# Two seven-product blocks per MLP, with weights split two pieces at a time

## The chip, the cores and the metric

The kernel runs on one core of one Trainium2 chip. The metric is device time in microseconds (us) of one execution; lower is better. Before the change three runs gave 847.58, 847.60 and 848.07 us, median 847.6. The engines are PE (matrix products), DVE (element-wise on tiles), ACT (element-wise with functions), POOL, and SP, which here only issues transfers.

## What is computed

A two-layer encoder on 256 tokens of 1024 channels, all in float32. Each layer has a token mixer (pooling, dilated attention, gates) and a gated MLP; only the MLP is touched in depth:

```python
def _conv_ffn(xn, w_up, conv_w, conv_b, w_down):
    a, gval = jnp.split(xn @ w_up, 2, axis=-1)          # 256 x 1024 times 1024 x 5632
    a = depthwise_conv_width_3(a, conv_w) + conv_b       # neighbours along the tokens
    return (jax.nn.gelu(a) * gval) @ w_down              # 256 x 2816 times 2816 x 1024

for layer in range(2):
    h = h + _token_mixer(_rmsnorm(h, norm1[layer]), ...)
    h = h + _conv_ffn(_rmsnorm(h, norm2[layer]), ...)
```

## The kernel before

**Precision by splitting.** Products run on 32-bit operands in a rounded format. To keep float32 accuracy every weight piece is split in two: ACT copies the raw piece into `wh` (rounded), DVE subtracts, `wl = raw - wh`. A product of a piece is then three products: x-high by wh, x-high by wl, x-low by wh. A *piece* is 128 x 1024 elements, half of a 1 MB load of one raw buffer. There are three raw buffers (`RAW`) and five pairs of split buffers (`BUFS`).

**Class Weights** holds the list of loads and the list of pieces in the order in which PE uses them. `get()` hands PE the next piece and first calls `_split` for the pieces up to four ahead, as far as split buffers are free. A split is ACT's copy, then whatever waits in `W.between` (DVE work of the moment), then DVE's subtraction. `load` issues a transfer on SP's queue, up to three raw buffers ahead; that transfer waits on the queue until its buffer is free. `bring_back` issues the second half of a crossing (below), right after the next weight load.

**The MLP's groups.** `w_up` has 5632 columns: branch a (2816) and branch g (2816), in groups of 512 columns, ("a", n) and ("g", n), n = 0 to 4, and a last group ("b", 20) with 256 of each. A plain group has 4 pieces, each with 12 products of 128 x 512 (`by_tokens`, `v_sum`). `w_down` is used in 22 pieces, also 12 products each (`residual_mm`, "d"). The order is that of `MLP_GROUPS`.

**The block ("w", 3)** computes a3 and g3 together. The 2 x 2 arrangement of (weight half, branch) needs eight products of quadrants; Strassen's identity makes it seven: 11, T1, 22, T2, 21, T3, T4, each in two units of 6 products of 128 x 512 (`halves_of_block`). T1 to T4 are differences of quadrants that DVE makes in place in the raw tile (`use_block`, L344), before they are split. Between them stand units "d" (`BLOCK`). DVE adds the banks afterwards (`add`, L1692).

**Crossings.** Convolution needs channels on partitions and tokens along the row. `to_z`/`turn` transpose a group's two results on DVE (two instructions at L852), `send` writes them to DRAM (L857), and four reads (L864) bring them back in the other layout.

**Convolution.** For each pair of 128-channel chunks f = 0, 2, ..., 20 five steps run: `fetch_up` (6 ACT instructions), `neighbours` (2 DVE), `activate` (ACT, gelu), `gate` (DVE), `keep_up` (ACT copy, then a DVE subtraction). Chunks f and f+1 belong to group f // 4. A *place* is one unit of PE work, counted through the MLP; place 8 is the first unit after the groups a0 and g0. `PAIR_PLACES` gives (p1, p3) for each f: `fetch_up` at p1, `neighbours` and `activate` at p1 + 1, `gate` and `keep_up` at p3. `at_place` puts `neighbours` and `gate` into `W.between`: if the unit of that place splits a piece, they run on DVE between ACT's copy and DVE's subtraction, else after the unit. The ACT steps and the end of `keep_up` come behind the unit.

From place 8 on the MLP is in a hand-written order (`manual_schedule`): every engine takes its instructions in the order in which the program names them.

Of the kernel before, what the change touches and what calls it, by code (L numbers as in the profile page):

```python
# [52 lines left out]
    ("11", 0), ("11", 1), "d", ("T1", 0), ("T1", 1), "d", "d", ("22", 0), ("22", 1), "d", ("T2", 0), ("T2", 1), "d",  # L53
    ("21", 0), ("21", 1), "d", ("T3", 0), ("T3", 1), "d", "d", ("T4", 0), ("T4", 1),
# [64 lines left out]
class Weights:  # L119
# [6 lines left out]
    RAW, BUFS, LOOK = 3, 5, 3  # L126

    def __init__(self, tc, pool, idle, small):
# [7 lines left out]
        self.between = []  # L136
# [3 lines left out]
        self.sums = {}  # L140

    def add(self, src, shape, cuts, tag=None):

        n = len(self.loads)
        self.loads.append((src, shape, tag))
        return [(n, cut, c_shape) for cut, c_shape in cuts]

    def use(self, pieces, slots=()):
        slots = list(slots) + [None] * len(pieces)
        self.pieces += [p + (slot,) for p, slot in zip(pieces, slots)]  # L150

    def ahead(self, i):


        upto = min(n for n, *_ in self.pieces[i : i + 3])
# [52 lines left out]
    def _split(self, upto):  # L208
        nc = self.nc
        first = self.n_split  # L210
        while self.n_split < len(self.pieces):
            i = self.n_split
            n, cut, shape, slot = self.pieces[i]
            if i >= upto and (slot is None or i >= max(upto, first + 2) or i >= upto + 4 or i < 4):
                break
            if slot is None and len(self.live) == self.BUFS:
                break
            self.load(n + 1)
            with ExitStack() as queued:
                for insts, some in self.later:  # L220
                    for inst in insts if i in some else ():
# [6 lines left out]
                if i in self.sums:  # L228
                    self.sums.pop(i)()
            self.load(self.ahead(i))  # L230

    def run_between(self):

        while self.between:
            self.between.pop(0)()

    def open_next(self):
# [3 lines left out]
        n, cut, shape, slot = self.pieces[i]  # L241
        if slot is None:
            self.live.add(i)
            h, l = (
                self.pool.tile([P, *shape], F32R, tag=tag, bufs=self.BUFS, name=f"{tag}{i}")
                for tag in ("wh", "wl")
            )
# [44 lines left out]
    def free(self, i):  # L292
        self.live.discard(i)


@with_exitstack
def encoder(ctx, tc, x, w_in, w_pool, pool_scale, w_a, w_b, w_o, norm1, norm2, w_up, conv_w,
# [32 lines left out]
    def use_block(units, made, first):  # L330
# [9 lines left out]
        def sum_later(i, name, j):  # L340

            def make():
                one, other = terms[name]
                nc.vector.tensor_sub(out=raw(name, j), in0=raw(one, j), in1=raw(other, j))  # L344
# [3 lines left out]
        for j in range(2):  # L348
            sum_later(len(W.pieces) + first + j, "T1", j)
        behind = [u for u in units if len(u) > 2]  # L350
        for unit in units:
            if len(unit) > 2:
                W.use([unit])
                behind = behind[1:] or behind
                continue
            name, j = unit
            if name in SUMS:
                sum_later(len(W.pieces), SUMS[name], j)
            if name in ("22", "21"):
                W.use([made[name][j]])  # L360
            else:
                W.use([(behind[0][0], lambda t, name=name, j=j: raw(name, j), (2, 512))])

    def first_quadrants(w, n):
        return {
            "11": quadrant(w, 0, DFF + n * 512, "ybig"), "12": quadrant(w, 0, n * 512, "at2"),
        }

    def block(w, down, n, made):
        made = dict(made)  # L370
        d = rows(down, 0) + rows(down, 2 * P)
        made["22"] = quadrant(w, 1, n * 512)
        d += rows(down, 4 * P)
        made["21"] = quadrant(w, 1, DFF + n * 512)
        d += rows(down, 6 * P)
# [1391 lines left out]
```

## Time and profile before

| | |
|---|---|
| median of three runs | 847.6 us |
| the profiled execution's own time | 848.11 us |
| its span, first to last instruction | 846.3 us |
| MLP of layer 0, from the group g0 on | about 257.6 to 425 us |
| MLP of layer 1, from the group g0 on | about 673.9 us to the end |
| granted TensorE clock | 0.999 |
| transfers | 214.02 MB, 253 GB/s |

The page of the profile gives busy time for each engine and the chain of work that ended last. The view by windows gives the busy time of each engine in chosen stretches; the timeline lists instructions in order, with the idle time before each and what ended it; the view of waits sums that up. Two consecutive instructions of an engine overlap in the trace by about 0.1 us, so what an instruction costs in a full queue is the distance between starts and not its length.

### The profile page before, as it was taken

To read this page: it belongs to the slowest core of one execution; us is meant where nothing else is said; L and a number is where in the kernel's file an instruction comes from. 1 tells how busy PE (TensorE), PEld (TensorE's weight loads), DVE (VectorE), ACT (ScalarE), POOL (GpSimd) and SP (SyncE) were. 2 spreads that over 40 slices of the span, in tenths; PEclk is the share of its full clock that TensorE was granted. 3 is DMA by queue.
4 is the path that set the end of the run, shared out by engine and by line. 5 is a ranking of instruction groups with operands and counts; after the bars stand their busy time and mean duration, and the time that the engine had idled before them with its cause. 6 is when DMAs were issued, how large, how long until landed. Compare 5 with 4: busy or idle time off the path is not lost.

```text
span 846.3 us, 10959 instructions
## 1 busy us (share of the span) xinstructions
PE 838.7 (99%) x3889; PEld 699.3 (83%) x3889; DVE 665.5 (79%) x860; ACT 531.1 (63%) x770; POOL 35.5 (4%) x96
## 2 busy tenths in 40 slices
PE   9999999999999999999999999999999999999997
PEld 7888888888888887888888888888888888888886
DVE  6968877757767799788898997868577867998884
ACT  7744556655554776488765555577455647757883
POOL 1720000000010000000000000000000100000000
PEclk9999999999999999999999999999999999999999
DMA  8699987796759886889857669968777499768861
GB/s 305 211 304 289 317 282 251 246 282 218 233 206 302 276 275 199 256 264 316 272 185 225 222 225 316 284 235 261 247 261 269 164 308 309 227 224 275 303 218 50
DMA packets 147967, 214.02 MB, mean 253 GB/s; under 512 B 7801, under 2 KB 69185, under 8 KB 147913
## 3 DMA queue, kind: packets, MB, share of 16 engines
q1 hardware_dynamic: 147480, 212.67, 76.8%
q10 hardware_dynamic: 432, 0.66, 0.2%
q8 instruction: 30, 0.49, 0.2%
q14 instruction: 25, 0.20, 0.1%
HBM read 186.02 MB, written 27.28 MB: 252 GB/s over the span
## 4 chain that ended last, share of the span: by engine, by line
PE 90%; DMA 3%; DVE 3%; ACT 2%; issue 1%; POOL 0%; ACTq 0%; SPq 0%; DVEq 0%; POOLq 0%
PE t_ps L798 54%; PE res_ps L716 6%; PE res_ps L715 6%; PE res_ps L717 6%; PE t_ps L917 4%; PE v_ps L798 3%; DMA raw<-in_w_up_dram 3%; PE v_ps L1101 3%; PE v_ps L917 2%; PE pool_ps L702 1%; PE v_ps L1000 1%; PE o_ps L1392 1%; PE s_ps L1344 1%; ACT wh L259 1%; DVE wl L261 1%; PE s_ps L1339 1%
## 5 line engine op out<-in xcount | busy, mean ns | idle before, releaser
L261 DVE TENSOR_TENSOR wl<-raw,wh 128x1024 fp32r<-128x1024 f32 x292 | 350.9, 1219 | 92.4 <-ACT wh L259 91.7
L798 PE MATMUL t_ps<-wh,x 128*128 128x512 f32 x1280 | 401.8, 390 | 0.0
L259 ACT CAST wh<-raw 128x1024 fp32r<-128x1024 f32 x292 | 302.1, 1048 | 158.8 <-PE t_ps L798 71.2
L798 PEld LDWEIGHTS t_ps<-wh,x 128*128 128x128 f32 x1280 | 240.3, 188 | 50.0
L798 PE MATMUL t_ps<-wl,x 128*128 128x512 f32 x640 | 249.0, 389 | 0.0
L798 PEld LDWEIGHTS t_ps<-wl,x 128*128 128x128 f32 x640 | 120.2, 188 | 24.7
L715 PE MATMUL res_ps<-wh,actq 128*128 128x512 f32 (+1 forms) x184 | 70.0, 380 | 0.0
L716 PE MATMUL res_ps<-wl,actq 128*128 128x512 f32 (+1 forms) x184 | 69.8, 380 | 0.0
L717 PE MATMUL res_ps<-wh,actk 128*128 128x512 f32 (+1 forms) x184 | 69.3, 380 | 0.0
L798 PE MATMUL t_ps<-wh,po 128*128 128x512 f32 x128 | 41.4, 395 | 0.0
L715 PEld LDWEIGHTS res_ps<-wh,actq 128*128 128x128 f32 x184 | 34.6, 188 | 6.7
L716 PEld LDWEIGHTS res_ps<-wl,actq 128*128 128x128 f32 x184 | 34.6, 188 | 6.7
L717 PEld LDWEIGHTS res_ps<-wh,actk 128*128 128x128 f32 x184 | 34.6, 188 | 6.5
L1604 ACT ACTIVATE a<-zga,prm 128x256 f32<-128x256 f32 x80 | 38.9, 512 | 0.0
L592 POOL TENSOR_SCALAR ss<-ss 128x1 f32<-128x1 f32 x8 | 3.1, 386 | 764.2 <-ACT junk L585 764.2
L344 DVE TENSOR_TENSOR raw<-raw,raw 128x1024 f32<-128x1024 f32 x24 | 29.3, 1222 | 0.0
L798 PEld LDWEIGHTS t_ps<-wh,po 128*128 128x128 f32 x128 | 24.0, 188 | 4.9
L715 PE MATMUL res_ps<-wh,m 128*128 128x512 f32 (+1 forms) x72 | 26.5, 368 | 0.0
L716 PE MATMUL res_ps<-wl,m 128*128 128x512 f32 (+1 forms) x72 | 26.3, 365 | 0.0
L717 PE MATMUL res_ps<-wh,m 128*128 128x512 f32 (+1 forms) x72 | 26.0, 365 | 0.0
L1608 DVE TENSOR_TENSOR y<-y,a 128x510 f32<-128x510 f32 x22 | 14.9, 679 | 13.6 <-ACT y L1602 13.6
L798 PE MATMUL t_ps<-wl,po 128*128 128x512 f32 x64 | 24.9, 390 | 0.0
(221 smaller groups left out, 1069.6 us busy)
## 6 DMA issues: line engine op xcount, KB each, us to landing
raw<-in_w_in_dram SPq DMA_DIRECT2D x58, 1024.0 KB
raw<-in_w_up_dram SPq DMA_DIRECT2D x40, 1024.0 KB
raw<-in_w_down_dram SPq DMA_DIRECT2D x22, 1024.0 KB
crossing<-crossing SPq DMA_DIRECT2D x22, 512.0 KB
crossing<-way SPq DMA_DIRECT2D x16, 512.0 KB
raw<-in_w_a_dram SPq DMA_DIRECT2D x8, 1024.0 KB
raw<-in_w_o_dram SPq DMA_DIRECT2D x8, 1024.0 KB
zga<-crossing SPq DMA_DIRECT2D x40, 128.0 KB
```

The lines of the kernel that those rows point to most:

```text
L259: inst = nc.scalar.copy(out=h, in_=src)
L261: inst = self.rests[i] = nc.vector.tensor_sub(out=l, in0=src, in1=h.bitcast(F32))
L344: nc.vector.tensor_sub(out=raw(name, j), in0=raw(one, j), in1=raw(other, j))
L702: nc.tensor.matmul(out, w(k), x, start=(steps is first and k == 0), stop=(steps is last and k == nk - 1), skip_group_check=turns["rest"],)
L715: nc.tensor.matmul(ps, ah, wh, start=first, stop=False, skip_group_check=on)
L716: nc.tensor.matmul(ps, ah, wl, start=False, stop=False, skip_group_check=on)
L717: nc.tensor.matmul(ps, al, wh, start=False, stop=last, skip_group_check=on)
L798: nc.tensor.matmul(ps, x2[:, 2 * n + j, part, t, :], w[:, j, :], start=(n + m == 0), stop=(n == last and m == 5),)
L917: nc.tensor.matmul(ps, operands[name](part, 2 * j + c), w[:, c, :], start=(name in ("11", "T1") and j + m == 0), stop=(j == 1 and m == 5), ...
L1101: nc.tensor.matmul(ps[t], a[:, k, t, :], w[:, j, :], start=(k + m == 0), stop=(k == KD - 1 and m == 2),)
L1604: nc.scalar.mul(out=out, in_=a, mul=row(j, c))
L1608: nc.vector.tensor_add(out=y[:, :, 1:], in0=y[:, :, 1:], in1=t["a0"][:, :, : S - 1])
```

## The change

Per MLP there are two blocks, groups 1 and 3, in place of one; the groups g2 and b run inside the first, the first eight pieces of `w_down` inside the second. Two pieces of the same load are split by one ACT and one DVE instruction of 128 x 2048 (`W.two`). There are six split slots in place of five, taken in neighbouring pairs. A load is issued when a raw buffer is given back, not ahead of that, and the quadrants of the second block are loaded once those of the first are used up (`not_before`). The sums T1 to T4 are made whole. In the block, ACT's copies of banks come ahead of a split (`at_once`). The places of the convolutions change. The bias table of the attention holds two heads at a time and is loaded again for the other two.

```diff
 MLP_GROUPS = (
-    ("g", 0), ("a", 1), ("g", 1), ("a", 2), ("g", 2), ("w", 3), ("b", 20), ("a", 4), ("g", 4),
-    ("d", 8), ("d", 12), ("d", 16), ("d", 20),
+    ("g", 0), ("a", 2), ("w", 1), ("a", 4), ("w", 3), ("g", 4), ("d", 8), ("d", 12), ("d", 16), ("d", 20),
 )
+BETWEEN = {1: (("g", 2), ("b", 4 * NQ)), 3: (("d", 0), ("d", 4))}

 PAIR_PLACES = (
-    (11, 14), (14, 16), (19, 22), (21, 23), (46, 48), (49, 51), (52, 54), (55, 57), (60, 62), (63, 65), (58, 60),
+    (9, 13), (11, 15), (35, 38), (41, 45), (22, 25), (26, 29), (60, 64), (63, 66), (65, 69), (68, 71), (70, 73),
 )

 BLOCK = (
-    ("11", 0), ("11", 1), "d", ("T1", 0), ("T1", 1), "d", "d", ("22", 0), ("22", 1), "d", ("T2", 0), ("T2", 1), "d",
-    ("21", 0), ("21", 1), "d", ("T3", 0), ("T3", 1), "d", "d", ("T4", 0), ("T4", 1),
+    ("11", 0), ("11", 1), "d", "d", ("T1", 0), ("T1", 1), "d", "d", ("22", 0), ("22", 1), "d", "d",
+    ("T2", 0), ("T2", 1), "d", "d", ("T3", 0), ("T3", 1), ("21", 0), ("21", 1), ("T4", 0), ("T4", 1),
 )
...
-    RAW, BUFS, LOOK = 3, 5, 3
+    RAW, SLOTS, LOOK = 3, 6, 3
...
     def ahead(self, i):
+        if self.two:
+            upto = end = self.n_loaded
+            held = sum(
+                tag is None and self.last_use[n] > i
+                for n, (_, _, tag) in enumerate(self.loads[:upto]) if n > upto - 10
+            )
+            while held < self.RAW and end < len(self.loads) and self.not_before.get(end, i) <= i:
+                end += 1
+                if self.loads[end - 1][2] is None:
+                    held += 1
+                    upto = end
+            return upto
...
     def _split(self, upto):
...
+            count = 1
+            if self.makes_two(i):
+                if self.two_slots() is not None:
+                    count = 2
+                elif i >= self.n_got + 2:
+                    break
...
-                for hi, lo, *_ in self.open_next():
+                for hi, lo, *_ in self.open_next(count):
+                    self.run_at_once()
                     hi()
                     self.run_between()
                     lo()
...
     def open_next(self, count=1):
...
+            if count == 2:
+                h, l = (s[:, at : at + 2].rearrange("p s c -> p (s c)") for s in self.slots)
+                src = whole(self.raw[n]).rearrange("p k c -> p (k c)")
+                self.n_split += 2
+                def both(n):
+                    if n == 0:
+                        return nc.scalar.copy(out=h, in_=src)
+                    inst = nc.vector.tensor_sub(out=l, in0=src, in1=h.bitcast(F32))
...
-                nc.vector.tensor_sub(out=raw(name, j), in0=raw(one, j), in1=raw(other, j))
+                nc.vector.tensor_sub(out=whole(name), in0=whole(one), in1=whole(other))
...
+                if kind2 == "w":
+                    name, tag, c0 = (("11", "ybig", DFF), ("12", "at2", 0))[j]
+                    if corner:
+                        W.not_before[len(W.loads)] = W.last_use[corner[name][0][0]]
+                    made[name] = quadrant(w_up[l], 0, c0 + n2 * 512, tag)
...
-    bt = const.tile([P, HPG, NT * P], F32, name="bt")
+    bt = const.tile([P, 2, NT * P], F32, name="bt")
...
+    def load_bias(first, queue=nc.sync):
...
+        else:
+            visits["u", 1, 2] = ((load_bias, 0),)
...
-            4: ((W.bring_back,), (scores, 1)),
+            4: ((W.bring_back,), (scores, 1), (load_bias, 2, nc.scalar)),
...
         def at_place(p, make, *first):
+            W.at_once = [step for step in first if step in by_scalar]
+            first = [step for step in first if step not in by_scalar]
...
             def add(t):
                 m = kept["m"][:, t]
                 nc.vector.tensor_add(out=m, in0=bank("q"), in1=m)
-                turn("a", t, m)
+
+            def add_last():
+                add(1)
+                for t in range(2):
+                    turn("a", t, kept["m"][:, t])
+
+            by_scalar.extend((keep_first, keep_fifth, keep_both))
             after = {
                 "11": (keep_first,), "T1": (keep_fifth,), "22": (keep_both,), "T2": (lambda: add(0),),
-                "T3": (lambda: add(1),), "T4": (lambda: turn("g", 0, bank("p")), lambda: turn("g", 1, bank("q"))),
+                "T3": (add_last,), "T4": (lambda: turn("g", 0, bank("p")), lambda: turn("g", 1, bank("q"))),
             }
```

After an entry of `BLOCK` has been computed, the steps that `after` names for it run in the next unit. In the new order, places 8 to 11 are a2, 12 to 33 the first block, 34 to 37 a4, 38 to 59 the second block, 60 to 63 g4, and 64 on the pieces of `w_down` from the eighth.

More of the change, by code (lines that the diff above doesn't have):

```diff
@@ L140, in __init__ @@
         self.sums = {}
+        self.slots = [pool.tile([P, self.SLOTS, 1024], F32R, tag=tag, name=tag) for tag in ("wh", "wl")]
+        self.freed = {slot: slot - self.SLOTS for slot in range(self.SLOTS)}
+        self.slot_of, self.n_freed = {}, 0
     def add(self, src, shape, cuts, tag=None):
@@ L227, in _split, with run_at_once, makes_two @@
                     lo()
-                if i in self.sums:
-                    self.sums.pop(i)()
-            self.load(self.ahead(i))
+                for j in range(i, i + count):
+                    if j in self.sums:
+                        self.sums.pop(j)()
+            self.load(self.ahead(i + count - 1))
+    def run_at_once(self):
+        while self.at_once:
+            self.at_once.pop(0)()
     def run_between(self):
+        self.run_at_once()
         while self.between:
             self.between.pop(0)()
-    def open_next(self):
+    def makes_two(self, i):
+        if not self.two or i < self.n_scaled or i + 1 >= len(self.pieces):
+            return False
+        (*_, whole, slot), (*_, whole2, slot2) = self.pieces[i : i + 2]
+        return slot is None and slot2 is None and bool(whole) and whole2 is False
@@ L1545, in encoder @@
         run(attended)
-        g1 = gain(norm1[l + 1] if l + 1 < DEPTH else norm_f)
+        W.two = True
         acts = {}
```

163 lines of the change are left out of this document (99 added, 64 removed), and 10 rows, old and new, of the table VALUES.

## The prediction, as recorded before the run

> **What bounds the kernel now.** I read the page first: engine shares, then the chain that ended last.
>
> ```profile
> span 846.3 us, 10959 instructions
> PE 838.7 (99%) x3889; PEld 699.3 (83%) x3889; DVE 665.5 (79%) x860; ACT 531.1 (63%) x770; POOL 35.5 (4%) x96
> PE 90%; DMA 3%; DVE 3%; ACT 2%; issue 1%; POOL 0%; ACTq 0%; SPq 0%; DVEq 0%; POOLq 0%
> ```
>
> PE is busy almost throughout, but its lengths overlap, so this alone doesn't prove that it is never late. The chain in order of time gives the real pace:
>
> ```profile
> 438.30 5.44 PE t_ps L798 x24
> 443.74 1.36 PE v_ps L917 x6
> ```
>
> 24 products take 5.44 us: 0.2267 us each. A plain unit of 12 costs 2.72 us, a block unit of 6 costs 1.36. Then the windows: g0 to block, block, behind it, in layer 0.
>
> ```profile
> 257.60:317.60 60.00, 60.00 (x265) 49.36 (x263) 47.31 (x55) 39.63 (x57) 0.00 (x0) 1.00 0.89 293
> 317.60:358.70 41.10, 40.69 (x180) 33.62 (x180) 36.62 (x36) 22.59 (x25) 0.00 (x0) 1.00 0.70 225
> 358.70:417.50 58.80, 58.80 (x262) 48.70 (x262) 49.24 (x59) 50.71 (x82) 0.00 (x0) 1.00 0.87 282
> ```
>
> Columns are the stretch, its length, PE, PEld, DVE, ACT, POOL (busy and count), clock, DMA share, GB/s. 265 products at 0.2267 are 60.1 us: the first stretch is full, and so is the third. The block holds 180 products, 40.8 of 41.1 us. So PE sets the time everywhere in the MLP, and nothing that only makes loads or splits earlier can gain: the one gap is at the block's start, in PE's timeline:
>
> ```profile
> 318.03 0.47 PE L917 MATMUL t_ps<-wh,sx 128*128 128x512 f32 x1 [0.41 <-DVE crossing L852]
> ```
>
> But DVE is 89% busy in the block (36.6 of 41.1). That decides below.
>
> **The change, part by part.**
>
> *Products.* A group pair costs 96 products, as a block 84. One more block per MLP removes 12 x 0.2267 = 2.72 us, two MLPs 5.44 us. All are on the path.
>
> *What DVE and ACT pay.* What the vector queue did in the old block, and the distances between starts in full queues:
>
> ```profile
> L261 DVE TENSOR_TENSOR wl<-raw,wh 128x1024 fp32r<-128x1024 f32 x22 | 25.8, 1215 | 1.6 <-ACT wh L259 1.5
> L344 DVE TENSOR_TENSOR raw<-raw,raw 128x1024 f32<-128x1024 f32 x6 | 7.3, 1221 | 0.0
> ...
> 301.76 1.22 DVE L344 TENSOR_TENSOR raw<-raw,raw 128x1024 f32<-128x1024 f32 x1
> 302.89 1.22 DVE L261 TENSOR_TENSOR wl<-raw,wh 128x1024 fp32r<-128x1024 f32 x1
> ...
> 314.24 0.68 DVE L1625 TENSOR_TENSOR actk<-g,actq 128x512 fp32r<-128x512 f32 x1
> 314.84 0.69 DVE L1616 TENSOR_TENSOR g<-y,zg 128x512 f32<-128x512 f32 x1
> ```
> ```profile
> 309.35 0.52 ACT L1604 ACTIVATE a<-zga,prm 128x256 f32<-128x256 f32 x1
> ...
> 311.97 1.03 ACT L259 CAST wh<-raw 128x1024 fp32r<-128x1024 f32 x1
> 312.91 0.61 ACT L1624 CAST actq<-g 128x512 fp32r<-128x512 f32 x1
> 313.42 0.63 ACT L1612 ACTIVATE y<-y 128x512 f32<-128x512 f32 x1
> 313.96 1.04 ACT L259 CAST wh<-raw 128x1024 fp32r<-128x1024 f32 x1
> ```
>
> DVE pays 1.13 us for 1024 elements a partition and 0.60 for 512; 512 more cost 0.53, so an instruction of 2048 should cost 1.13 + 1.06 = 2.2 us (between 2.1, no fixed part, and 2.26, two single ones; nearest is the slope). ACT pays 0.94 for 1024 and 0.51 for 512, so 1.8 for 2048; `fetch_up` is 2.6 us (309.35 to 311.97), gelu 0.54. A split of two pieces is then 1.8 on ACT and 2.2 on DVE, and merging saves under 0.1 us a pair.
>
> The Trainium skill, "VectorE: DVE Perf Modes", section "The TRN2 errata", gives (N+151)/0.96 ns for such an instruction: 1.22 us at 1024, as the trace's lengths say, and 2.29 at 2048. By these lengths merging would save 0.16 us a pair; the distances above show that a full queue hides about half of that.
>
> *The first block (places 12 to 33).* PE needs 84 + 96 products, 40.8 us. The DVE queue holds: 11 splits of pairs (7 of the block, 4 of g2 and b), 24.2; the sums T2, T3, T4, 6.6; and 24 instructions of 512 at 0.6: transposes of a2, g2, b and a1 (8), two additions, and of the convolutions f0 `gate` and end (2), f2, f8 and f10 four each (14). That is 14.4, together 45.2 us in 40.8. The old block had no convolution step in it: the window's rows are splits, sums, transposes and two additions.
>
> How far may DVE be behind? Six slots are three pairs: the split of a pair can begin when PE has left the pair three before, and must end two pairs later, 2.72 + 5.44 = 8.2 us in the block. ACT and DVE take 4.0 of it, so the slack is about 4 us, and at the end, where T3, 21 and T4 stand without a plain unit between, 5.44 - 4.0 = 1.4. Without any idle time DVE reaches the first split of a4, due at 40.8, after 45.2 - 2.2 = 43.0 us, and it starts 1.0 late (the sum T1 ends 1.8 + 2.2 + 2.2 = 6.2 us into a unit pair of 5.44, with two latencies): **a stall of 3.2 us at least.**
>
> DVE will not be free of idle time. An odd place splits nothing, so there `neighbours` or `gate` stands behind the last split on DVE, gelu or the copy of `keep_up` waits for it on ACT, the next split's copy stands behind that on ACT, and DVE waits for this copy. The trace shows the knot once already, harmlessly:
>
> ```profile
> 307.87 0.64 ACT L1612 ACTIVATE y<-y 128x512 f32<-128x512 f32 x1 [2.78 <-DVE y L1609]
> 308.41 1.04 ACT L259 CAST wh<-raw 128x1024 fp32r<-128x1024 f32 x1
> ```
> ```profile
> 309.48 1.23 DVE L261 TENSOR_TENSOR wl<-raw,wh 128x1024 fp32r<-128x1024 f32 x1 [0.50 <-ACT wh L259]
> ```
>
> ACT sat 2.78 us until the neighbours were added; DVE then waited for ACT's copy. f0 and f2 have their gate at odd places (13, 15), f8 and f10 both steps (23 and 25, 27 and 29). At the end of the block, from the start of the unit before T3: copy of 21 1.8, rest 2.2, sum T4 2.2, neighbours of f10 1.2, gelu 0.6, copy of T4 1.8, rest 2.2, gate 0.6, copy 0.6, its rest 0.6, addition of T3 0.6. T4 needs that addition, for it accumulates in the same bank. The sum is 14.4 us; PE has 5.44 + 2.72 + 2.72 = 10.9: 3.5 late even with a punctual start. Following the order from T2 on, with f8's steps ahead, T4 is some 8 late and a4 9; with the lateness that f0 and f2 leave (T1 to d), 13. I take 11 us, between 9 and 13; bounds 3.2 and 17 (second rival).
>
> *a4 and the second block.* DVE has 9.0 of 10.9 us, then 38 of 40.8, for of convolutions only f6 and the end of f4 stand in it. The chain at its end without a convolution is 1.8 + 2.2 + 2.2 + 1.8 + 2.2 + 0.6 = 10.8 of 10.9, so T4 comes about in time. f4 and f12 are fetched 5 and 4 places behind the sending of a1 and a3; a crossing's reads were all issued 5.4 us after its send:
>
> ```profile
> 348.40 0.37 SPq L857 DMA_DIRECT2D crossing<-crossing  x1
> ...
> 351.69 2.12 SPq L864 DMA_DIRECT2D zga<-crossing  x4
> ```
>
> For f4 that fits, for f12 ACT waits a few us within its slack. I take 2 us (0 to 4).
>
> *The tail.* From g4 on DVE has 9 splits of pairs (19.8), five convolutions (12) and four transposes (2.4), 34 us, in 10.9 + 14 x 2.72 = 49 of PE: nothing lost, for the slack is the plain one, 2 x 5.44 - 4.0. The new places gain nothing, since PE had no gap there.
>
> *The rest.* In layer 1's value block 42 instructions on DVE become 21 of double size: 1.4 us less on an engine with 80 of 90 us; slack as above, but no step more than before: nothing, at most 3 lost. Reloading the bias puts 5 transfers on ACT's queue, some 2.2 us at 0.45 each (as the reads above), where ACT is busy 30.5 of 50 us (attention): nothing, at most 2 per layer.
>
> ```profile
> 145.00:195.00 50.00, 50.00 (x275) 43.26 (x274) 34.17 (x58) 30.47 (x50) 0.00 (x0) 1.00 0.79 251
> 438.00:528.00 90.00, 90.00 (x399) 74.53 (x398) 80.20 (x101) 51.68 (x61) 0.00 (x0) 1.00 0.72 230
> ```
>
> **The sum** per MLP: -2.72 + 11 + 2 = +10.3; two MLPs +20.6. From the profiled execution's 848.1 that is 868.7, and from the median, 0.5 lower, **868 us.**
>
> **Rivals.**
>
> *Faster: the product count decides.* If DVE and ACT stay within their slack of 4 us in places 12 to 33, only -5.44 is left: 842. For it speaks that the old block ran with DVE at 89% and PE hardly waited; against it, that the new one asks 45.2 of 40.8. It would hold if the queue needed under about 41 us, that is, if seven of the small steps weren't there. The Trainium skill, "Perfetto Trace Analysis", section "Identifying the Most-Contended Engine", would optimize the engine with the highest occupancy first; here that is PE on average, and the product count would be the gain. The windows show that the average doesn't hold in the block.
>
> *Slower still: reads behind a load.* g2's crossing is sent at place 20, and its reads come back only behind the next load. At places 20 and 22 nothing is given back or the load must wait for T3; the first load is the second block's 11, at place 24, which waits on SP for T3's split to end. Then four reads (1.8 us) and their landing, and `gate` of f8, place 25, stands first on DVE: some 4 us more. First block 17, the rest 4: -2.72 + 21 = 18.3 per MLP, 884.
>
> *No change:* DVE's bare 3.2 us and no idle time: +0.5 per MLP, 848.6.
>
> **Chances.** About 0.2% (1.7 us) is what a measurement of this kernel can tell from no change. Forecast, anywhere from 853 to 878: 0.63; still slower, 884: 0.12; so slower 0.75. No change 0.09. Faster, 842: 0.16. The range 846 to 885 leaves out the faster case and what lies above the slowest.
>
> **What would show it.** Right: PE gaps of several us in each MLP between the unit before T3 and a4's first piece, ended by DVE (split, or addition L1692); DVE near 100% busy or waiting for ACT's copy through places 12 to 33; the tail and attention without gaps; DVE instructions of 128 x 2048 2.2 us apart; `gate` of f8 waiting on zg in the second rival. Wrong: block 1 in about 41 us, or gaps in the tail. An error of the 2.2 us by 0.1 moves the block by 1.4 us; more than that would come from slots freed in another order than I read.

## The result and the profile after

| | before | after |
|---|---|---|
| median of four runs, us | 847.82 (847.58 to 848.07) | 932.77 (931.46 to 935.05) |
| the profiled execution, us | 848.11 | 935.05 |

The changed kernel is slower by 85 us: the ratio is 1.1005, with a 95% interval of 1.0979 to 1.1031. Forecast were +20.6 us; the time lies outside the range. First the page of the kernel after: its span, the engines, and the granted clock in 40 slices.

```profile
span 933.3 us, 10667 instructions
...
PE 862.2 (92%) x3865; PEld 707.3 (76%) x3865; DVE 690.7 (74%) x771; ACT 529.6 (57%) x687; POOL 35.4 (4%) x96
...
PEclk9999999999999879999999999999999988789999
```

There are 24 products fewer (3889 to 3865), as counted, and yet PE is busy for longer, with dents in the clock at two places: the two MLPs. The view by windows, first and second block of layer 0, then of layer 1 (columns as before):

```profile
280.80:346.80 66.00, 46.68 (x182) 36.88 (x181) 47.47 (x39) 32.40 (x36) 0.00 (x0) 0.84 0.57 175
357.70:410.10 52.40, 45.44 (x181) 35.71 (x180) 41.98 (x29) 29.71 (x28) 0.00 (x0) 0.93 0.52 172
742.40:811.30 68.90, 48.66 (x181) 38.50 (x180) 48.81 (x40) 34.22 (x40) 0.00 (x0) 0.83 0.55 165
822.20:874.20 52.00, 45.30 (x182) 35.77 (x180) 42.02 (x29) 29.29 (x27) 0.00 (x0) 0.93 0.53 170
```

Each row holds 180 products, 40.8 us of work. The first blocks take 25 and 28 us more, the second ones 11 to 12 each, 76 us in all. The span grew by 87 although the products that are gone save 5.4, so some 16 us more came elsewhere, most of them behind the blocks. VectorE's work in the first block is about what the forecast said (45.2 us; it was busy for 47.5), but it stood still for 18.5 of the 66 us. Where PE waited longest in that block, from its timeline:

```profile
327.89 0.77 PE L1014 MATMUL v_ps<-wh,sx 128*128 128x512 f32 x1 [10.65 <-DVE kept L1794]
...
341.65 0.77 PE L1014 MATMUL v_ps<-wh,x 128*128 128x512 f32 x1 [5.67 <-DVE kept L1794]
```

These are the first products of T3 and of T4. Both wait for VectorE's addition; what it was doing before the first of them, from VectorE's timeline:

```profile
315.18 2.29 DVE L312 TENSOR_TENSOR wl<-raw,wh 128x2048 fp32r<-128x2048 f32 x1 [2.50 <-ACT wh L311]
325.08 0.69 DVE L1715 TENSOR_TENSOR g<-y,zg 128x512 f32<-128x512 f32 x1 [7.61 <-DMA zg<-crossing]
...
327.06 0.68 DVE L1794 TENSOR_TENSOR kept<-v_ps,kept 128x512 f32<-128x512 f32 x1
```

Nothing at all: the `gate` of f8 waited 7.61 us for the reads of group g2's crossing, and the addition stood behind it. The reads, on SP's queue:

```profile
304.74 0.37 SPq L954 DMA_DIRECT2D crossing<-crossing  x1
317.50 0.37 SPq L199 DMA_DIRECT2D raw<-in_w_up_dram  x1
317.96 2.14 SPq L961 DMA_DIRECT2D zg<-crossing  x4
```

The crossing was written at 304.74; its reads come only behind the next load, and that load waits for a quadrant whose last use, T3's subtraction, ends at 315.18 + 2.29 = 317.47. So they are issued 13.2 us after the write.

In the second block PE's two longest waits (1.82 us before 363.13, 2.83 before 373.31) lead back to the crossings of a1 and g1. On SP's queue, then ScalarE and VectorE waiting for them (the `fetch_up` and the `gate` of f4):

```profile
342.75 0.38 SPq L954 DMA_DIRECT2D crossing<-crossing  x1
344.92 0.37 SPq L199 DMA_DIRECT2D raw<-in_w_down_dram  x1
351.22 1.80 SPq L961 DMA_DIRECT2D zga<-crossing  x4
353.12 0.45 SPq L199 DMA_DIRECT2D raw<-in_w_up_dram  x1
353.67 0.45 SPq L954 DMA_DIRECT2D crossing<-crossing  x1
363.10 0.37 SPq L199 DMA_DIRECT2D raw<-in_w_down_dram  x1
363.57 2.10 SPq L961 DMA_DIRECT2D zg<-crossing  x4
```
```profile
356.24 0.53 ACT L1703 ACTIVATE a<-zga,prm 128x256 f32<-128x256 f32 x1 [7.32 <-DMA zga<-crossing]
```
```profile
370.37 0.69 DVE L1715 TENSOR_TENSOR g<-y,zg 128x512 f32<-128x512 f32 x1 [3.87 <-DMA zg<-crossing]
```

The rounding that the first wait ends with stands behind the one, the split of T1 behind the other. The view of crossings says who waited for their data in the whole kernel (us, times): the kernel after, then the kernel before, which has no row for `fetch_up` (a) or for the transposes (crossing):

```profile
  DVE g L1715: 28.9, 8
  ACT a L1703: 27.9, 4
  DVE crossing L949: 8.0, 3
```
```profile
  DVE g L1616: 1.7, 2
```

### The profile page after: what moved, and what is told of

It is laid out like the page before. It is cut to its first block, busy times and chain, and to the rows that moved or that the text cites. A ratio compares the mean times of both kernels' runs of the same rounds, so it can differ in the third digit from the quotient of the medians.

```text
span 933.3 us, 10667 instructions
## 1 busy us (share of the span) xinstructions
PE 862.2 (92%) x3865; PEld 707.3 (76%) x3865; DVE 690.7 (74%) x771; ACT 529.6 (57%) x687; POOL 35.4 (4%) x96
## 4 chain that ended last, share of the span: by engine, by line
PE 47%; DMA 18%; DVE 18%; ACT 9%; issue 4%; SPq 3%; POOL 0%; DVEq 0%; ACTq 0%; POOLq 0%
PE t_ps L895 31%; DVE wl L312 7%; DMA crossing<-crossing 6%; DMA zg<-crossing 5%; ACT wh L311 4%; PE v_ps L895 3%; DVE raw L424 2%; PE v_ps L1198 2%; PE v_ps L1014 2%; DMA raw<-in_w_up_dram 2%; SPq L961 2%; PE pool_ps L799 1%; DMA raw<-in_w_o_dram 1%; PE v_ps L1097 1%; DVE g L1715 1%
## 5 line engine op out<-in xcount | busy, mean ns | idle before, releaser
L895 PE MATMUL t_ps<-wh,x 128*128 128x512 f32 x1152 | 365.1, 392 | 1.6 <-ACT wh L311 1.6
L312 DVE TENSOR_TENSOR wl<-raw,wh 128x2048 fp32r<-128x2048 f32 x101 | 230.1, 2283 | 58.0 <-ACT wh L311 58.0
L895 PEld LDWEIGHTS t_ps<-wh,x 128*128 128x128 f32 x1152 | 217.6, 189 | 47.4 <-ACT wh L311 2.0
L311 ACT CAST wh<-raw 128x2048 fp32r<-128x2048 f32 x101 | 192.0, 1906 | 86.0 <-PE t_ps L895 30.0
L895 PE MATMUL t_ps<-wl,x 128*128 128x512 f32 x576 | 226.1, 393 | 5.0 <-DVE wl L312 4.8
L335 DVE TENSOR_TENSOR wl<-raw,wh 128x1024 fp32r<-128x1024 f32 x102 | 121.3, 1218 | 36.2 <-ACT wh L333 36.1
L333 ACT CAST wh<-raw 128x1024 fp32r<-128x1024 f32 x102 | 104.6, 1047 | 25.7 <-PE t_ps L895 14.2
L1014 PE MATMUL v_ps<-wh,sx 128*128 128x512 f32 x96 | 35.0, 428 | 21.5 <-DVE kept L1794 21.5
L424 DVE TENSOR_TENSOR raw<-raw,raw 128x2048 f32<-128x2048 f32 x20 | 45.7, 2284 | 0.0
L1014 PE MATMUL v_ps<-wh,x 128*128 128x512 f32 x72 | 27.1, 440 | 11.6 <-DVE kept L1794 11.6
L1715 DVE TENSOR_TENSOR g<-y,zg 128x512 f32<-128x512 f32 x20 | 13.7, 686 | 28.9 <-DMA zg<-crossing 28.9
```

Of the source, the lines that this page charges most:

```text
L311: return nc.scalar.copy(out=h, in_=src)
L312: inst = nc.vector.tensor_sub(out=l, in0=src, in1=h.bitcast(F32))
L333: inst = nc.scalar.copy(out=h, in_=src)
L335: inst = self.rests[i] = nc.vector.tensor_sub(out=l, in0=src, in1=h.bitcast(F32))
L424: nc.vector.tensor_sub(out=whole(name), in0=whole(one), in1=whole(other))
L895: nc.tensor.matmul(ps, x2[:, 2 * n + j, part, t, :], w[:, j, :], start=(n + m == 0), stop=(n == last and m == 5),)
```

## The experiments

Eighteen kernels, one run each beside a run of the kernel before on the same chip (847.4 to 849.8 us). Line numbers shift by up to four between them. The lengths of the blocks are those of the same 180 products in each trace, in layer 0. They are surer than the totals: the stage from the norm of layer 1 to the next norm, which no experiment but e18 edits, takes from 236.9 (e4) to 241.1 us (e9) in the other traces, so a few us between two totals need not come from the edit.

| kernel | us | first block | second block |
|---|---|---|---|
| after (profiled execution) | 935.05 | 66.0 | 52.4 |
| e1: reads at place 22 | 917.86 | 58.1 | 51.6 |
| e8: e1, single splits | 907.52 | 53.4 | 51.9 |
| e5: reads, steps at even places | 894.68 | 47.0 | 51.9 |
| e10: e5, T1 split singly | 897.31 | 48.7 | 52.3 |
| e9: e5, two sums on GpSimd | 926.32 | 54.2 | 59.0 |
| e12: e5, reads at every place | 890.40 | 47.7 | 47.4 |
| e13: e12, f8 and f10 behind the first block | 891.54 | 41.9 | 54.9 |
| e16: e13, loads held at three places | 884.57 | 41.9 | 50.2 |
| e17: e16, single splits | 877.65 | 40.9 | 50.2 |

### The reads, the places, the pairs: e1, e2, e3

e1 issues the reads that are held back ahead of the unit of place 22:

```diff
+            if p == 22:
+                W.bring_back()
             r = make()
```

> The changed kernel, but the four reads of g2's crossing are issued on SP before the unit of place 22, no longer behind the load of the second block's first quadrant. Theory R (the gate of f8 waits for reads that stand behind that load, and the half-speed clock that the wait brings with it): the 10.7 us gap before T3 falls to about 3 us and the clock stays up there, 8 + 2.5 us per MLP, about 912 us. Theory P (the DVE and ACT queues of the first block are overfull, whoever feeds the gate): T3 waits for the addition all the same, at least 925 us.

917.86 us. The wait before T3 fell from 10.65 to 2.97 us: the second rival's mechanism is shown, and it is worth some 15 us in all (17 against the profiled execution). T4 waits longer than before, from PE's timeline of e1:

```profile
321.80 0.47 PE L1014 MATMUL v_ps<-wh,sx 128*128 128x512 f32 x1 [2.97 <-DVE kept L1796]
335.56 0.77 PE L1014 MATMUL v_ps<-wh,x 128*128 128x512 f32 x1 [8.05 <-DVE kept L1796]
```

e2 moves the steps of f8 and f10 into the second block:

```diff
-    ... (22, 25), (26, 29), ...
+    ... (46, 49), (58, 62), ...
```

> The changed kernel, but the convolutions of f8 and f10 stand at places (46, 49) and (58, 62), in the second block and behind it, not in the first. Theory P: the first block falls from 66 and 69 us to 41 to 46, the second block and g4 pay some 5 us: about 885 to 895 us. Theory R alone, in which only the gate of f8 is to blame and the steps of f10 cost nothing: 911 us or more, with the 5.7 us gap before T4 still there.

918.65 us. In e2 the two convolutions read the tile into which a4's crossing has come by then, not group 2's data. The first block shrank to 45.9 us, the second grew to 64.4. It shows the first block without these steps, but is no clean test of the total.

e3 splits one piece at a time from place 8 on, with no other edit:

```diff
-        if not self.two or i < self.n_scaled ...
+        if not self.two or self.single or i < self.n_scaled ...
```

> The changed kernel, but from place 8 on every piece is split by itself, 128 x 1024, with the same six slots and the same loads. Theory G (pairs leave every second place without a split, so that a step there stands between two splits with ACT and DVE waiting for each other in turn): the gaps in the first block shrink by half or more, about 890 to 905 us. Theories P and R: the same work in the same queues, and the same reads: 925 to 945 us.

900.48 us. In e3 loads come at other places, and the reads with them, so that the `gate` of f8 is placed ahead of the reads of its own data and doesn't wait for them. What is left of the 32 us gain for the pairs alone can't be told from this run; e8 does that.

### The order of the small steps: e5; the pairs: e8

The forecast named a knot at odd places, where no split is made: ScalarE waits for VectorE's small step, and the next rounding stands behind it. e5 lets all of VectorE's steps up to f10 fall on even places, and issues the reads at places 21 and 22:

```diff
-    (9, 13), (11, 15), (35, 38), (41, 45), (22, 25), (26, 29), ...
+    (9, 14), (11, 16), (35, 38), (41, 46), (21, 26), (27, 30), ...
...
+            if p in (21, 22):
+                W.bring_back()
```

> The changed kernel with g2's reads brought back early (before places 21 and 22) and with the places of the first six convolutions moved by one at most so that each neighbour step and each gate stands at an even place, where a split goes with it: (9, 14), (11, 16), (35, 38), (41, 46), (21, 26), (27, 30) for f0, f2, f4, f6, f8, f10. The same work in the same block. Theory K (a step at an odd place makes ACT's and DVE's queues wait for each other in turn): the gap before T4 falls from 8.2 to 2 us or less and that before T3 from 3.1 to 1: about 890 to 898 us, against 918 with the reads alone. Theory P (the sum of the work alone): the gaps move but their sum stays: 910 to 918 us.

894.68 us: 23 us below e1 with the same instructions in the first block. Its length fell from 58.1 to 47.0 us. That the reads come one place earlier isn't the reason: the `gate` of f8 waits for them in neither kernel. The windows of the first block, e1 and then e5:

```profile
282.70:340.80 58.10, 44.44 (x181) 35.26 (x181) 47.45 (x39) 32.44 (x36) 0.00 (x0) 0.92 0.63 200
```
```profile
281.10:328.10 47.00, 43.71 (x181) 35.40 (x180) 45.56 (x39) 32.67 (x36) 0.00 (x0) 0.94 0.75 234
```

VectorE is now busy for nearly the whole stretch: the idle time is gone, the excess of work is left. e8 is e1 with single splits in the MLP:

```diff
+            if p == 22:
+                W.bring_back()
...
+        if not self.two or self.single or i < self.n_scaled ...
```

> The changed kernel with g2's reads brought back before place 22 and with single splits from place 8 on. Theory G: 890 to 900 us, against 918 with pairs. Theories P and R: 915 to 925 us, for the work and the reads are those of the run with the reads alone.

907.52 us, 10 below e1 and between the two expectations. It fits that a step waits less behind a shorter split, though loads come at other places, too; it is no replacement for the order.

### The clock: e6

PE's clock was granted at half speed for some 66 us of the kernel after (T3 took 5.2 us in place of 2.72). e6 puts 40 products that nobody reads before T3 and 20 before T4 of the first block, while PE would wait:

```diff
+    for m in range(count):
+        nc.tensor.matmul(ps, x2[:, 0, 0, 0, :], ..., start=(m == 0), stop=(m == count - 1))
```

> The changed kernel with products that nobody reads in the first block of each MLP: 40 of 128 x 512 ahead of T3 and 20 ahead of T4, 9.1 and 4.5 us at full speed, less than PE waits there. They write a bank of their own. Theory C (after a wait PE runs at half speed for some us, which costs 2.4 us behind each of the two gaps): T3 and the products behind T4 run at 0.227 us each and the time falls by 8 to 10 us, to about 923 us. If the slow products have another cause: no less than 931 us.

933.93 us, as before, though the time at half speed fell to 35 us. Mean clock, after and then e6:

```profile
core 0: 933.3 us, clock 0.965
```
```profile
core 0: 932.1 us, clock 0.982
```

So the slow clock is mostly an effect: what e6 took away of it brought no gain that can be measured. Behind the wait VectorE and ScalarE, not PE, set the pace: the addition that T4 waits for starts 13.76 us after the one that T3 waits for in both kernels (327.06 and 340.82; 329.69 and 343.45 in e6). The slow products that e6 leaves weren't tried.

### One block only: e4, e7, e11

e4 has the groups and places of the kernel before (one block), with everything else changed:

```diff
-    ("g", 0), ("a", 2), ("w", 1), ("a", 4), ("w", 3), ("g", 4), ...
+    ("g", 0), ("a", 1), ("g", 1), ("a", 2), ("g", 2), ("w", 3), ("b", 20), ("a", 4), ("g", 4), ...
...
-    (9, 13), (11, 15), (35, 38), (41, 45), (22, 25), (26, 29), (60, 64), ...
+    (11, 14), (14, 16), (19, 22), (21, 23), (46, 48), (49, 51), (52, 54), ...
```

> The changed kernel with the old list of groups and the old places: one block per MLP, group 3, with d0 and d4 in it; pairs, slots, load rule, sums, bias and the new order inside the block stay. If the second block with its convolutions is the cause: 846 to 856 us. If the pairs or the load rule cost by themselves: over 865 us.

867.93 us: 18 us slower than the kernel before on the same chip, without any second block. e7 adds single splits and reads at every place:

```diff
+            W.bring_back()
             r = make()
...
+        if not self.two or self.single or i < self.n_scaled ...
```

> One block per MLP as in the earlier one-block run (868 us), but with single splits from place 8 on, and reads of crossings brought back at each place. Theory G (splitting in pairs is what costs the one-block kernel its 18 us over the kernel before): 848 to 854 us. If the load rule, the order inside the block or the bias cost it: still over 860 us.

871.29 us. The block takes 45.3 us (e4: 46.5), and new waits of 1 to 1.5 us stand in the last convolutions. e11 is e4 with T1 alone split half by half:

```diff
-    False if j else lambda t, name=name: whole(name),
+    False if j or mlp and name == "T1" else lambda t, name=name: whole(name),
```

> The one-block kernel e4_oneblock (867.9 us) with T1 alone split half by half. Theory H: the wait of 2.1 us before the low products of T1, and the half clock behind it (together some 4 us in each MLP), go: 860 to 863. Theory M (what makes the one-block kernel 18 us slower than before isn't the pair at T1 but the order of loads and many small waits): 866 to 869.

862.45 us, 5.5 less, 4.0 of it in the two MLPs. The first low product of T1, in the timelines of PE, e4 and then e11:

```profile
327.10 0.80 PE L1015 MATMUL t_ps<-wl,sx 128*128 128x512 f32 x1 [1.83 <-DVE wl L313]
```
```profile
323.06 0.50 PE L1015 MATMUL t_ps<-wl,sx 128*128 128x512 f32 x1 [0.42 <-DVE wl L336]
```

A pair hands over its first half only when both halves are subtracted; behind a sum, where nothing has been made in advance, PE waits for that. e10 is the same edit on e5, where VectorE is full:

```diff
+    False if j or mlp and name == "T1" else lambda t, name=name: whole(name),
```

> On top of e5_even (894.7 us), T1 alone is split half by half in both blocks; everything else stays in pairs. Theory H (a pair hands over its first half only when both are rounded and subtracted: the low products of the first half wait for it, 3.3 us before T1 of the second block in each MLP): that wait falls to about 2, the time to 889 to 892. Theory D (VectorE's time is the bound): two halves cost 0.2 us more than a pair, so no gain, 894 to 896.

897.31 us: no gain, as the theory of a full VectorE said, though the wait at T1 of the second block fell from 3.3 to 2.0 us in layer 0.

### Less work for VectorE: e9, e13

e9 gives the sums of T2 and T3 to GpSimd:

```diff
+    engine = nc.gpsimd if mlp and name in ("T2", "T3") else nc.vector
+    engine.tensor_sub(out=whole(name), in0=whole(one), in1=whole(other))
```

> On top of e5_even (894.7 us), the differences for T2 and T3 of each MLP block are taken by GpSimd instead of VectorE: 2 x 2.28 us less for VectorE in each of the four blocks, 18.2 us in all. Theory D (VectorE's time is the bound in the blocks: it was busy 21.5 of 22.0 us around T3 and T4 in e5_even, and 47.5 us of work stood against 40.8 us of products in the kernel after): the wait before T4 (3.45 us) falls below 1.5 and the time to 878 to 888. Theory L (GpSimd's work is paid for by VectorE, whose own two-input operations stretch while it runs, or the difference comes so late that its split waits): 893 or more, with splits that begin later than in e5_even. Theory K (only the order of the steps counts, not the sum): 892 to 896.

926.32 us, 32 above e5. GpSimd's timeline in e9, then VectorE's in the same stretch:

```profile
287.33 9.52 POOL L425 TENSOR_TENSOR raw<-raw,raw 128x2048 f32<-128x2048 f32 x2 [36.74 <-DMA zg<-crossing]
```
```profile
288.16 4.33 DVE L1716 TENSOR_TENSOR g<-y,zg 128x512 f32<-128x512 f32 x1 [0.91 <-DMA zg<-crossing]
292.41 6.59 DVE L312 TENSOR_TENSOR wl<-raw,wh 128x2048 fp32r<-128x2048 f32 x1
```

GpSimd's two sums end at 291.94 and 296.85. VectorE's instruction of 512 takes 4.33 us in place of 0.69 and ends 0.6 us behind the first; that of 2048 takes 6.59 in place of 2.29 and ends 2.2 us behind the second. The work was not shared; VectorE waited. In the four blocks it was busy for 190.8 us, against 175.4 in e5, with 18.2 us of work less.

e12 is e5 with the reads at every place:

```diff
-            if p in (21, 22):
-                W.bring_back()
+            W.bring_back()
```

> On top of e5_even (894.7 us), the reads of every crossing are issued at the next place of the hand-written part instead of at the next load. In e5_even ScalarE waited 8.4 us for the data of the third convolution's fetch at place 35 (reads issued 8.9 us after their write), with the rounding of the second block's first product queued behind it, and VectorE 4.2 us at the gate of that convolution (reads 9.3 us after their write), with T1's subtraction behind it. Theory R (held reads): both waits go below 1 us, PE's waits of 1.1, 2.1 and 3.3 us at the start of the second block shrink to about 2 in all, and the time is 880 to 886. Theory D (VectorE's demand): the waits move, the time stays at 892 to 896. Theory Q (reads that wait at the head of SP's queue for their write now delay the loads behind them): over 896.

890.40 us, 4.3 less where 9 to 15 were expected, between the two theories: the second blocks fell by 4.5 and 5.2 us (to 47.4 in layer 0), but the stretches behind them, from d8 on, grew by 3.3 and 1.5, and `fetch_up` still waited for crossed data, 32.3 us in four waits. e13 then takes group 2's convolutions out of the first block, and with them their work on VectorE:

```diff
-    (35, 38), (41, 46), (21, 26), (27, 30), ...
+    (37, 41), (43, 46), (31, 35), (34, 37), ...
```

> On top of e12_all_reads, the convolutions of group 2 leave the first block for the four places between the blocks: their steps go from places 21, 26 and 27, 30 to 31, 35 and 34, 37, and the third and fourth convolutions from 35, 38 and 41, 46 to 37, 41 and 43, 46. Theory D (VectorE is full from T2 to T4 of the first block, 21.5 of 22.0 us): the wait before T4 (3.4 us in each MLP) and the half clock behind it go, 10 to 16 us below e12_all_reads. Theory K (only the order counts, and e12_all_reads has it right): within 3 us of it. If the moved steps crowd the second block instead: above it, with new waits at T1 of that block.

891.54 us. The first block, from e13's windows, has its products' length plus 1 us; the second is up from 47.4 to 54.9:

```profile
281.40:323.30 41.90, 41.08 (x182) 33.70 (x180) 39.39 (x30) 27.54 (x26) 0.00 (x0) 1.00 0.76 241
334.60:389.40 54.80, 45.94 (x181) 35.77 (x180) 46.50 (x36) 33.04 (x34) 0.00 (x0) 0.94 0.56 182
```

With 39.4 us of work in 41.9, VectorE holds nothing up; the moved steps hold up the second block. Theory D held for the first block and the crowding for the second; the sum gained nothing.

### Loads in front of a crossing: e16, e17

SP's timeline of e13 around T3's crossing:

```profile
319.73 0.37 SPq L199 DMA_DIRECT2D raw<-in_w_up_dram  x1
320.20 2.27 SPq L961 DMA_DIRECT2D zb<-crossing  x4
322.51 0.45 SPq L199 DMA_DIRECT2D raw<-in_w_down_dram  x1
323.06 0.41 SPq L954 DMA_DIRECT2D crossing<-crossing  x1
323.71 0.37 SPq L199 DMA_DIRECT2D raw<-in_w_down_dram  x1
331.90 1.80 SPq L961 DMA_DIRECT2D zga<-crossing  x4
```

Two loads of 1 MB stand just ahead of the write, one just behind it, and it takes 8.8 us until its reads can start. VectorE's transposes of T4, which use the same tile, waited 4.70 us for it. e16 issues no load at places 27 to 29:

```diff
+HOLD = (27, 28, 29)
...
+            if self.hold:
+                return self.n_loaded
...
+            W.hold = p in HOLD
```

> On top of e13_late (891.5 us), no load is issued at places 27 to 29 of the hand-written part, so that T3's crossing of the first block goes to the DMA queues ahead of the loads of 1 MB that came just before it (in e13_late loads were issued at 319.7, 322.5 and 323.7 us around the write at 323.1, whose data had landed only at 331.9, 8.8 us later, and VectorE's transposes of T4 waited 4.7 us for it; in the kernel before, the write at 318.5 was followed by its reads after 4.1 us). Theory B (loads that are issued at once when a buffer is given back bunch in front of the crossings): the write lands within 6 us, the 4.7 us wait and the fetch's wait of 6.9 us fall below 2, PE's waits of 1.8 and 2.1 us at the first product of the second block to about 2 in all: 882 to 887. Theory D (VectorE's and ScalarE's work): no change within 2 us. If the held loads are late themselves: above 893, with roundings that wait for raw data.

884.57 us, as theory B said. The same write and reads in e16:

```profile
322.62 0.38 SPq L958 DMA_DIRECT2D crossing<-crossing  x1
323.10 0.41 SPq L203 DMA_DIRECT2D raw<-in_w_up_dram  x1
327.27 1.80 SPq L965 DMA_DIRECT2D zga<-crossing  x4
```

4.65 us instead of 8.8, and the transposes of T4 no longer wait for it. The second block of layer 0 became 4.7 us shorter, that of layer 1 only 0.9. e17 adds single splits:

```diff
+        if not self.two or self.single or i < self.n_scaled ...
```

> e16_hold with half-by-half splits in the MLP's hand-written part. Theory G (a pair makes the in-order queues coarse): 5 us or more below e16_hold, as e15_singles stood 4.9 us below e14_tail; then the best version with two blocks is some 878 us, still behind the kernel before. If pairs cost nothing any more once the loads are spread: within 2 us of e16_hold.

877.65 us, the best kernel with two blocks. Its first block, from its windows, has no wait left:

```profile
281.50:322.50 41.00, 41.00 (x182) 33.73 (x181) 38.98 (x40) 26.11 (x33) 0.00 (x0) 1.00 0.72 235
333.40:383.60 50.20, 43.91 (x182) 34.41 (x181) 43.66 (x43) 34.06 (x45) 0.00 (x0) 0.97 0.67 226
```

### The tail and the attention: e14, e15, e18

e14 puts the last convolution from (70, 73) to (58, 61). The tiles for its result are still to be read as chunks 8 and 9 there, so those products of `w_down` take chunks 20 and 21 twice; the instructions are the same.

```diff
-    ..., (68, 71), (70, 73),
+    ..., (68, 71), (58, 61),
```

> On top of e13_late, the last convolution of the MLP (whose data lie ready since the first block) goes from places 70, 73 to 58, 61, ahead of the tail. In e5_even the norm behind the tail began 3.2 us late, with VectorE's last products of the convolutions ending 3 us before it. Theory D: four convolutions instead of five stand in the last ten places; the norm's wait of 3.2 us in the first layer shrinks to below 1.5 and the tail of the second layer by as much, 3 to 6 us below e13_late. Rival (the steps now knot at T4 of the second block): a wait of over 2 us there, no gain or a loss.

884.68 us, 6.9 below e13; from d8 on it is 5.4 us shorter in layer 0 and 1.5 in layer 1. Five convolutions in the last ten places were too many, though the gain can't be had in this form. e15 is e14 with single splits, and with the same chunks exchanged:

```diff
+        if not self.two or self.single or i < self.n_scaled ...
```

> On top of e14_tail, all splits of the MLP's hand-written part are made half by half (1024 elements) instead of two at once. Theory G (a pair makes the in-order queues coarse: a step behind it waits 2.3 us instead of 1.2): 5 to 10 us below e14_tail, as e8_single stood 10 us below e1_reads. Theory D: more instructions for the same elements, 1 to 3 us above e14_tail.

879.79 us, 4.9 below e14. e18 switches pairs and the new rule of loads off in the attention of e17, too:

```diff
-                W.two = n != 1 or kind == "u"
+                W.two = False
```

> e17_hold_single (877.7 us) with pairs and the new rule of loads switched off in the attention's products as well (the value block, queries and keys), so that they stand only in the projections behind them. In the kernel after, the stages outside the MLP were 1.4 and 3.9 us longer than before. Theory A (pairs and loads cost this in the attention): 872 to 875, with those two stages back within 1 us of before. Rival (it comes from the reloaded bias or the smaller slots): 877 to 879.

885.33 us, 7.7 above e17: theory A falls. From the norm of layer 1 to the next one the trace has 239.5 us in e17, 243.8 in e18 and 236.3 in the kernel before. Without pairs and the new rule the stage got no shorter, so what it lost comes from something else. That the two help there isn't shown: the two MLPs, which e18 doesn't edit, are 1.9 and 2.0 us longer as well.

## Why the forecast was wrong

Its direction was right, and so was the kind of reason: the first block asks VectorE for more than its 40.8 us, and small steps knot its queue with ScalarE's. The sizes were not, and waits in other stretches were put at nothing.

*Products and instruction prices* held: 24 products fewer, VectorE's instructions of 2048 start 2.20 us apart in a full queue (299.00 and 301.20 in its timeline), ScalarE's 1.8.

*The first block* was put at 11 us; it is 25 and 28. The mechanisms were named, their sizes not: the reads behind a load, left to a rival with a chance of 0.12, cost 8 us in each MLP (66.0 to 58.1 us); the rival had 6. The order of the steps cost 11 and 13 more (58.1 to 47.0; 60.4 to 47.7 in layer 1), and the steps of f8 and f10 another 5 and 4 (to 41.9 and 43.3). Without the reads the forecast had 11 where these last two parts make 16 to 17. From T2 on it had T4 8 us late in all; in e1 T3 waits 2.97 and T4 another 8.05. Ahead of that it allowed some 4 us for what f0 and f2 leave, and e1 waits 1.5 before a piece of g2 and 1.5 before one of b. Of the 17.3 us by which e1's first block exceeds its products some 3 are left: products at half the clock, which the forecast didn't have.

*"Reads behind a load"* was in fact no alternative to the knots but stood on top of them: the load that carries the reads waits for T3's subtraction by the order of the program, and T3 waits 10.65 and 10.9 us in the two layers. It should have been in the sum.

*The second block* was put at 2 us; it is 11.6. The step that failed is "a crossing's reads were all issued 5.4 us after its send". That was read from the kernel before, and counts from the write to the end of the last read's issue. In the kernel after the same count gives 10.3 us for a1 (342.75 to 353.02), 12.0 for g1 (353.67 to 365.67), and 15.4 for g2 in the first block, for loads that are issued as soon as a buffer is given back stand in front of the write or delay the reads. e12 and e16 take back 4.5 and 4.7 us of it, in layer 0. The rest stays: even e17 takes 50.2 us there, and the steps of f8 and f10, once out of the first block, cost this one 7.4 us (e12 to e13).

*The tail and the rest* were put at nothing. The tail was 8 us longer in layer 0 and 3 in layer 1 (from the piece d8 on); five convolutions there in ten places were costed by VectorE's total (34 us in 49), the same way of counting that failed in the first block, and e14 takes back 5.4 and 1.5 us of it. The stage from the norm to the next norm in layer 1 was 3.5 us longer in the kernel after, and e18 doesn't bring it back by leaving out pairs and the load rule. The reloaded bias and the slots weren't tried alone.

*A window was misread.* The prediction's window of the old block began 5.6 us late, and it concluded that no convolution step stood in it. Its own lines at 314.24 and 314.84 are two such steps. The whole block (columns as before):

```profile
312.00:353.50 41.50, 41.09 (x181) 33.63 (x180) 39.70 (x41) 27.37 (x31) 0.00 (x0) 1.00 0.63 204
```

VectorE was busy for 39.7 of 41.5 us, and the block took only 0.7 us more than its products. So a nearly full VectorE is not what hurts. e13 and e17 say the same: 39 us of work in the first block and no wait. That is the condition that the faster rival gave, "if seven of the small steps weren't there", and in that block it came true.

*The faster rival as a whole* fails with e4 and e11: one block with all the other edits is already 14 to 18 us slower than before, about three times what the products of a second block bring. The prediction's sum had nothing for this; in e11 the two MLPs alone are 5.2 and 6.6 us longer than before. Of these edits only the pairs were tried by themselves, at T1 (e11); e7, with all splits single and the reads early, was no faster than e4. No version tried beats the kernel before (847.5); the nearest are e11 with one block (862.45) and e17 with two (877.65). What e17 still lacks, 30 us, is not settled: 9.4 and 9.0 us in the second blocks, and the rest in tail, attention and start. In the second blocks PE waits for the split of T1 (2.5 us), for that of a piece whose load came late (ScalarE waits 3.90 us for it) and for the addition before T4; which edit would remove these waits stays open.

## What to carry to other kernels

Count an in-order engine's work by the stretch that must hold it, and then follow each wait to what is queued behind it: a block that asked for a tenth too much lost more than half of its length, most of it (8 and 11 of 25 us) to reads behind a load and to the order of the steps. The latency of a transfer belongs to its place among the others, on the queue that issues it and on the DMA engines; it can't be carried over from a kernel that issues its loads at other times. When waits move but the time stays (e13, e10), the demand is what must be moved, to a stretch that has room.

## What the hardware showed beyond that

*VectorE stood while GpSimd made the sums.* The sums cost GpSimd 4.6 to 6.5 us each. In e9 they took 18.2 us of work off VectorE, and the kernel lost 32. The first of the two additions in `neighbours`, from the groups by line in e5 and then in e9 (busy us, mean ns):

```profile
L1707 DVE TENSOR_TENSOR y<-y,a 128x510 f32<-128x510 f32 x22 | 14.9, 679 | 17.4 <-ACT y L1701 17.4
```
```profile
L1708 DVE TENSOR_TENSOR y<-y,a 128x510 f32<-128x510 f32 x22 | 23.7, 1075 | 18.9 <-ACT y L1702 18.9
```

The Trainium skill, "Perfetto Trace Analysis", section "Optimizing Scalar/DVE Operations", says that the two share an SBUF read port and that moving work between them might not help. The trace agrees: subtractions of 2048 elements with both inputs in SBUF, the memory that holds the tiles, were held up for as long as 4.3 us (6.59 in place of 2.29).

*The clock fell in steps of some 3.4 us.* In or behind waits of 1.8 to 10.9 us, PE was granted half its clock for stretches of 3.4 to 13.7 us, 66 us in all (the last 5 at the kernel's end), and products then came 0.43 us apart. The Trainium skill, "TensorE: Matmul & The Clock Gate", Part 1, describes half rate after an idle window of about 3.4 us. The length of the steps agrees; the wait of 1.82 us before 363.13, with half the clock behind it, is shorter than that window. What e6 took away of the slow clock brought no time back.
